# First norm's modulation vectors: full-precision products with the weights stationary, in place of split products with the weights moving

## The chip, the cores and the metric

The kernel runs on one core of one Trainium2 chip. A core has TensorE (PE in the profile, its weight loads PEld), VectorE (DVE), ScalarE (ACT), GpSimd (POOL) and SyncE (SP), which issues most transfers here. The metric is the device time of one execution in microseconds (us); three runs of the kernel before gave 2555.66 to 2558.70 us, median 2557.21 us.

## What is computed

Two transformer blocks over 512 tokens of width 1024. The change lies at the very start of the first block, where two condition vectors (`c` and `c_ctx`, 1024 long each) become the shift and the scale of the first norm:

```python
sh1, sc1, g1, sh2, sc2, g2 = jnp.split(
    (jax.nn.silu(c) @ ada_w[layer] + ada_b[layer])[:, None, :], ADA_CHUNKS, axis=-1)
csh1, csc1, ... = jnp.split(jax.nn.silu(c_ctx) @ ada_w[layer] + ada_b[layer], ADA_CHUNKS, axis=-1)
h = modulate(rmsnorm(x, norm1_g[layer]), sh1, sc1)        # h * (1 + scale) + shift
hc = modulate(rmsnorm(ctx, norm1_g[layer]), csh1, csc1)
q, k, v, gu, gv, ga, gb = jnp.split(h @ w, IN_SPLITS, axis=-1)
```

Of the 6144 columns of `ada_w`, the first 2048 (sh1 and sc1) are used at this place, for both vectors. All later projections need `h`, so nothing of the main work can run before some of it is there. Everything is float32.

## The kernel before

Activations stand transposed: 8 blocks of 128 features, 512 tokens in the free dimension. A large float32 product is made of three products in the reduced type `float32r`: each operand is split into a high and a low part (`split`: ACT rounds, DVE subtracts), and `mm3` (L866 to L869) adds high by high (L867), low by high (L868) and high by low (L869).

The stage in question is the block under `p0` (L972 to L1024). It does three things at once, for feature blocks b = 0 to 7:

- `load(b)` brings 1 MB of ada weights (`ar`: 128 partitions, 8 blocks k of the contraction, 256 columns, which are block b's 128 shift columns and 128 scale columns), and splits it into `ah` and `al`: two instructions of 128x1024 on ACT (L925) and two on DVE (L926).
- `vectors(b, a)` multiplies. The stationary operand is `scp`, 128x4: the high and low parts of silu of the two vectors. The moving operand is 256 columns of `ah` or `al`; 16 products accumulate a 4x256 result (L987, L988). ACT copies it to `asb` (L990), two TensorE transposes turn it (L993), two DVE additions bring the parts and the bias together into `m` (L996, L997), and L998 makes the scale `s`. Then `modulated` makes block b of the activations: `md` on DVE (L947), `hh` on ACT (L948), `hl` on DVE (L949).
- The loop (L1017) multiplies block b of the activations with four weight blocks `wv` (the `gv` columns), 12 products of 512 columns for each b, accumulated over all eight b in four PSUM banks (`ps_mm`, `ps_S`). The four weights are split early by `early` (L1002; two subtractions on POOL, two on DVE).

In program order, vectors(0) and vectors(1) come ahead of the loop, and turn b of the loop holds vectors(b + 2). A scheduler interleaves the instructions of neighbouring turns on each engine, so the order that an engine really follows is shown with the change. Ahead of all stand the sums of squares of x (L913, L918) with two plain float32 products (L920, L922), from which `rfactor` makes the row factor `nR` (L893 to L899). Behind the loop, `gv` is activated from the four banks (L1065), and `proj` (L871) multiplies the next weights (L1071 on).

The buffers of `ar` are three. Further on, at L1045, the kernel makes eight small plain float32 products at a time: stationary a 128x128 block of `modacc`, moving the two columns of `one1`.

Of the kernel before, what the change touches and what calls it, by code (L numbers as in the profile page):

```python
# [8 lines left out]
F32 = mybir.dt.float32  # L9
F32R = mybir.dt.float32r  # L10
# [3 lines left out]
AF = mybir.ActivationFunctionType  # L14
ALU = mybir.AluOpType
# [3 lines left out]
P = 128  # L19
S = 512  # L20
D = 1024
KB = D // P
# [14 lines left out]
V_N1, V_N2, V_FG, V_MIX, V_FFN, V_LN, V_GN, V_AB, V_C, V_SINK = 0, 8, 16, 24, 32, 40, 44, 52, 100, 116  # L37
# [88 lines left out]
def pad(pool, size):  # L126

    pool.tile([P, size // 4], F32, name="pad", bufs=1)
# [695 lines left out]
def body(ctx, tc, I, out):  # L824
    nc = tc.nc
# [16 lines left out]
    vec = cp.tile([P, NVEC], F32, name="vec")  # L842
    nc.sync.dma_start(vec, I["vecs"])
    ident = cp.tile([P, P], F32, name="ident")
# [79 lines left out]
    def split(hi, lo, src):  # L924
        nc.scalar.activation(hi, src, AF.Copy)  # L925
        nc.vector.tensor_sub(lo, src, hi.bitcast(F32))  # L926
# [7 lines left out]
    with ExitStack() as c1:  # L934
        pa = c1.enter_context(tc.tile_pool(name="pa", bufs=1))
        bank = banks(T=(0, 1), mm=(2, 3), S=(4, 5), O=(6, 7))
# [27 lines left out]
        sc = pa.tile([P, KB, 2], F32, name="sc")  # L964
        cv = vec[:, V_C:V_C + 16].rearrange("p (k j) -> p k j", j=2)
        nc.scalar.activation(sc, cv, AF.Silu)
        scp = pa.tile([P, KB, 4], F32R, name="scp")
        split(scp[:, :, 0:2], scp[:, :, 2:4], sc)
        m1 = pa.tile([P, 2, 16], F32, name="m1")
        s1 = pa.tile([P, 2, KB], F32, name="s1")  # L970
        h = (hh, hl)
        with tc.tile_pool(name="p0", bufs=2, side="right") as p0:  # L972

            def load(b):
                ar = p0.tile([P, KB, 2 * P], F32, name="ar", bufs=3)
                nc.sync.dma_start(ar.rearrange("p k c -> p (k c)"), I["adaA"][b])
                ah = p0.tile([P, KB, 2 * P], F32R, name="ah", bufs=2)
                al = p0.tile([P, KB, 2 * P], F32R, name="al", bufs=2)
                for q in range(2):
                    k = slice(q * 4, q * 4 + 4)  # L980
                    split(ah[:, k], al[:, k], ar[:, k])
                return ah, al

            def vectors(b, a):
                acc = bank("O")[:4, :2 * P]
                for k in range(KB):
                    nc.tensor.matmul(acc, scp[:, k, :], a[0][:, k, :], start=k == 0, stop=False)  # L987
                    nc.tensor.matmul(acc[:2], scp[:, k, 0:2], a[1][:, k, :], start=False, stop=k == KB - 1)  # L988
                asb = p0.tile([4, 2, P], F32, name="asb", bufs=2)
                nc.scalar.activation(asb.rearrange("p j c -> p (j c)"), acc, AF.Copy)  # L990
                tp = bank("T")
                for j in range(2):
                    nc.tensor.transpose(tp[:, 4 * j:4 * j + 4], asb[:, j, :], ident[:4, :4])  # L993
                parts = tp[:, 0:8].rearrange("p (j h i) -> p h i j", j=2, h=2)
                m = m1[:, :, b::8]
                nc.vector.tensor_tensor(m, parts[:, 0], vec[:, V_AB + b:V_AB + 16:8].unsqueeze(1).broadcast_to([P, 2, 2]), ALU.add)  # L996
                nc.vector.tensor_tensor(m, m, parts[:, 1], ALU.add)  # L997
                nc.vector.scalar_tensor_tensor(s1[:, :, b], m[:, :, 1], 1.0, gain[:, V_N1 + b:V_N1 + b + 1].broadcast_to([P, 2]),  # L998
                                               op0=ALU.add, op1=ALU.mult)
                modulated(sp, hh, hl, lambda k: xT[:, k, :], S, s1[:, 0, :], R1, m1[:, 0, 0:8], (b,))  # L1000

            def early(b, pool):  # L1002
                raw = wp.tile([P, D], F32, tag="raw", name="raw", bufs=4)
                nc.sync.dma_start(raw, I["win"][b])
                wpool, n = (p0, 2) if b > 17 else (wp, 3)
                hi = wpool.tile([P, D], F32R, tag="hi", name="hi", bufs=n)
                nc.scalar.activation(hi, raw, AF.Copy)
                lo = wpool.tile([P, D], F32R, tag="lo", name="lo", bufs=n)
                (nc.gpsimd if pool else nc.vector).tensor_sub(lo, raw, hi.bitcast(F32))
                return hi, lo  # L1010

            gv_ps = [bank(tag) for tag in ("mm", "mm", "S", "S")]
            vectors(0, load(0))
            wv = [early(16, True), early(17, False)]
            vectors(1, load(1))
            wv += [early(18, True), early(19, False)]
            for b in range(KB):  # L1017
                if b + 2 < KB:
                    a = load(b + 2)
                c = slice(b * P, (b + 1) * P)  # L1020
                for acc, w in zip(gv_ps, wv):
                    mm3(acc, (w[0][:, c], w[1][:, c]), (hh[:, b, :], hl[:, b, :]), b == 0, b == KB - 1)
                if b + 2 < KB:
                    vectors(b + 2, a)  # L1024
# [43 lines left out]
        for b in range(4):  # L1068
            w = weight(I["win"][12 + b])
            acc = bank("mm")  # L1070
# [8 lines left out]
        for n in range(NT):  # L1079
            tp = bank("T")  # L1080
# [182 lines left out]
        x1 = mid.tile([P, KB, S], F32, name="x1")  # L1263
        with tc.tile_pool(name="pm", bufs=1) as pm, tc.tile_pool(name="sr2", bufs=1) as sr:

            pad(pm, 128)
            mh = pm.tile([P, KB, S], F32R, name="mh")
            ml = pm.tile([P, KB, S], F32R, name="ml")
            for b in range(KB):
                if b % 2 == 0:  # L1270
                    wa = weight(I["wpa"][b // 2])
                a_ps = bank("S")
                proj(a_ps, wa, (ya[:, 0], ya[:, 1]), 4, (b % 2) * 4)
                nc.vector.tensor_mul(sga[:, b, :], sga[:, b, :], a_ps)
                nc.vector.tensor_add(sga[:, b, :], sga[:, b, :], gbm[:, b, :])
                split(mh[:, b, :], ml[:, b, :], sga[:, b, :])
            ms, held, R = bank("T"), {}, mid.tile([P, S], F32, name="nR")

            def wout(b, w, c=slice(0, S)):
                acc = bank("mm")[:, :c.stop - c.start]  # L1280
                proj(acc, w, (mh[:, :, c], ml[:, :, c]))
                nc.vector.scalar_tensor_tensor(x1[:, b, c], acc, mod[:, 16 + b:17 + b], x1[:, b, c], op0=ALU.mult, op1=ALU.add)
                squares(sr, ms[:, c], b, x1[:, b, c], held, c)


            late = []
            for b in range(0, KB, 2):
                nc.scalar.dma_start(x1[:, b:b + 2, :], I["xT"][b:b + 2].rearrange("k p t -> p k t"))
            for b in range(KB):
                late.append((b, weight(I["wout"][b])))  # L1290
                if b < KB - 3:
                    wout(*late.pop())
            for half in HALVES:
                for a in late:
                    wout(*a, half)
                rfactor(sr, ms[:, half], S // 2, into=R[:, half], tag="h")
# [16 lines left out]
```

## Time and profile before

| | us |
|---|---|
| Median of three runs (lowest, highest) | 2557.21 (2555.66, 2558.70) |
| The profiled execution | 2557.7 |
| Its span | 2555.9 |
| PE busy | 2476.8 |
| PEld busy | 2135.9 |
| DVE busy | 1787.7 |
| ACT busy | 1065.5 |
| POOL busy | 309.1 |

A busy time is the union of an engine's instructions. Products are pipelined, so one record (0.28 or 0.39 us) is longer than the step from one to the next; what a product costs in a stream is read from the starts. The granted clock of TensorE is given as a share of 2.4 GHz: 1.00 is 2.4 GHz and 0.50 is 1.2 GHz. A view of the waits says what ended an engine's idle time. A plain float32 product leaves two records of a weight load and two of a product.

### The profile page before, as it was taken

How to read it: one execution, taken by the hardware profiler on the slowest of the kernel's cores; microseconds unless marked ns; L12 is line 12 of the kernel's file. 1: busy time of each engine (PE TensorE's matmuls, PEld its weight loads, DVE VectorE, ACT ScalarE, POOL GpSimd, SP SyncE). 2: the span in 40 equal slices, each digit the busy share in tenths (PEclk: the TensorE clock that was granted, in tenths of full speed). 3: DMA queues.
4: the chain of work that ended last, by engine and by line, in shares of the span. 5: the costliest groups of instructions: out<-in, count | busy, mean ns of one | idle time of the engine just before them, and what ended most of it. 6: DMA issues, size and time to landing. Idle time of an engine off the chain costs nothing.

```text
span 2555.9 us, 34576 instructions
## 1 busy us (share of the span) xinstructions
PE 2476.8 (97%) x13153; PEld 2135.9 (84%) x13153; DVE 1787.7 (70%) x2977; ACT 1065.5 (42%) x1846; POOL 309.1 (12%) x200
## 2 busy tenths in 40 slices
PE   7899999999899999999999999999999999999998
PEld 4788888888789999999988888886788888888887
DVE  6656745899989888878888888876854334533345
ACT  6524553433344444444444344344533323422343
POOL 0001100004331111123222222210000000000000
PEclk9999999999899999999999999999999999999999
DMA  6343433224667888799998899972112222222254
GB/s 240 128 173 128 159 106 118 103 83 169 218 245 277 300 294 295 288 347 332 339 344 322 310 358 361 359 292 99 58 50 83 91 101 97 94 96 99 101 182 162
DMA packets 145814, 511.28 MB, mean 200 GB/s; under 512 B 13680, under 2 KB 39408, under 8 KB 125936
## 3 DMA queue, kind: packets, MB, share of 16 engines
q1 hardware_dynamic: 114464, 330.14, 36.9%
q0 software_dynamic: 18432, 134.23, 14.1%
q10 hardware_dynamic: 12752, 44.70, 4.6%
q8 instruction: 103, 1.69, 0.3%
q14 instruction: 63, 0.52, 0.1%
HBM read 465.50 MB, written 43.52 MB: 199 GB/s over the span
## 4 chain that ended last, share of the span: by engine, by line
PE 84%; DVE 11%; issue 2%; ACT 2%; DMA 1%; POOL 0%; DVEq 0%; SPq 0%; ACTq 0%; POOLq 0%
PE ps_mm L867 13%; PE ps_mm L868 12%; PE ps_mm L869 12%; PE ps_o L869 7%; PE ps_o L868 7%; PE ps_o L867 7%; PE ps_S L867 3%; PE ps_S L868 3%; PE ps_S L869 3%; PE ps_S L197 3%; DVE lo L863 2%; PE ps_A L869 1%; PE ps_A L868 1%; PE ps_A L867 1%; PE ps_h L867 1%
## 5 line engine op out<-in xcount | busy, mean ns | idle before, releaser
L863 DVE TENSOR_TENSOR lo<-raw,hi 128x1024 fp32r<-128x1024 f32 x473 | 584.1, 1236 | 372.5 <-ACT hi L861 361.0
L861 ACT ACTIVATE hi<-raw 128x1024 fp32r<-128x1024 f32 x474 | 499.8, 1056 | 755.0 <-PE ps_mm L868 424.6
L869 PE MATMUL ps_mm<-hh,lo 128*128 128x512 f32 (+2 forms) x1784 | 654.5, 367 | 27.2 <-DVE lo L863 27.0
L867 PE MATMUL ps_mm<-hh,hi 128*128 128x512 f32 (+2 forms) x1784 | 661.4, 372 | 7.5 <-ACT gv L1065 2.4
L868 PE MATMUL ps_mm<-hl,hi 128*128 128x512 f32 (+2 forms) x1784 | 655.3, 367 | 2.4 <-DVE hl L926 2.2
L869 PEld LDWEIGHTS ps_mm<-hh,lo 128*128 128x128 f32 x1784 | 339.8, 190 | 65.3 <-DVE lo L863 30.2
L867 PEld LDWEIGHTS ps_mm<-hh,hi 128*128 128x128 f32 x1784 | 339.1, 191 | 45.5 <-ACT gv L1065 2.9
L868 PEld LDWEIGHTS ps_mm<-hl,hi 128*128 128x128 f32 x1784 | 340.1, 191 | 39.1 <-DVE hl L926 3.3
L178 POOL DMA_INDIRECT rows<-in_uv,dix x128 | 217.9, 1702 | 748.2 <-DVE act L427 190.0
L867 PE MATMUL ps_o<-hi,wh 128*128 128x512 f32 x768 | 298.9, 389 | 1.4 <-ACT wh L925 1.4
L869 PE MATMUL ps_o<-hi,wl 128*128 128x512 f32 x768 | 299.7, 390 | 0.6 <-DVE wl L926 0.5
L868 PE MATMUL ps_o<-lo,wh 128*128 128x512 f32 x768 | 299.2, 390 | 0.0
L172 DVE SCALAR_TENSOR_TENSOR rows<-rows,hn 128x1024 f32<-128x1024 f32 x128 | 159.9, 1250 | 18.6 <-ACT act L377 8.3
L869 PEld LDWEIGHTS ps_o<-hi,wl 128*128 128x128 f32 x768 | 144.1, 188 | 31.9 <-DVE wl L926 2.1
L169 DVE SCALAR_TENSOR_TENSOR accn<-rows,wgt,accn 128x1024 f32<-128x1024 f32 x128 | 167.2, 1306 | 4.4 <-ACT wgt L175 2.9
L867 PEld LDWEIGHTS ps_o<-hi,wh 128*128 128x128 f32 x768 | 144.2, 188 | 31.1 <-ACT wh L925 1.7
L868 PEld LDWEIGHTS ps_o<-lo,wh 128*128 128x128 f32 x768 | 144.1, 188 | 29.6
L925 ACT ACTIVATE wh<-act 128x384 fp32r<-128x384 f32 x104 | 54.7, 526 | 240.2 <-PE ps_o L868 219.1
L193 DVE TENSOR_TENSOR gi<-oh,gt 128x1536 bf16<-128x1536 bf16 x96 | 91.3, 954 | 0.9
L191 DVE TENSOR_TENSOR oh<-iob,ji 128x1024 bf16<-128x1024 bf16 x96 | 65.8, 688 | 26.8 <-PE ps_S L197 26.2
L197 PE MATMUL ps_S<-gi,oh 128*128 128x128 bf16 x1152 | 78.1, 219 | 0.0
L868 PE MATMUL ps_S<-hl,hi 128*128 128x512 f32 x200 | 78.0, 390 | 0.0
(398 smaller groups left out, 3589.2 us busy)
## 6 DMA issues: line engine op xcount, KB each, us to landing
raw<-in_uT SPq DMA_DIRECT2D x128, 512.0 KB
raw<-in_uv SPq DMA_DIRECT2D x128, 512.0 KB
raw<-in_win SPq DMA_DIRECT2D x82, 512.0 KB
raw<-in_wd SPq DMA_DIRECT2D x44, 512.0 KB
act<-act ACTq DMA_DIRECT2D x52, 384.0 KB
act<-act SPq DMA_DIRECT2D x52, 384.0 KB
gs<-stage ACTq DMA_DIRECT2D x16, 1152.0 KB
ring<-gs SPq DMA_DIRECT2D x12, 1536.0 KB
```

Source lines behind the costliest of these rows:

```text
L169: nc.vector.scalar_tensor_tensor(accn, rows.pop(k - 3)[:, D:], wgt[:, c], accn, op0=ALU.mult, op1=ALU.add)
L172: paced(nc.vector.scalar_tensor_tensor(r[:, :D], r[:, :D], 1.0, hn, op0=ALU.mult, op1=ALU.mult, accum_out=dot[:, c]))
L178: paced(nc.gpsimd.indirect_dma_start(out=r, out_offset=None, in_=I["uv"], in_offset=bass.IndirectOffsetOnAxis(ap=dix[:, k:k + 1], axis=0)))
L191: nc.vector.tensor_tensor(oh, io, each(ji[:, t0 // 4], 2), ALU.is_equal)
L193: nc.vector.tensor_tensor(gi, oh[:, 1].unsqueeze(1).broadcast_to([P, 3, 2, P, 2]), each(gt[:, t0 // 4], 3), ALU.mult)
L197: nc.tensor.matmul(g_ps[:, t, :], oh[:, 0, t // 2, :, t % 2], gi[:, j, t // 2, :, t % 2], start=j == 0, stop=j == 2)
L861: nc.scalar.activation(hi, raw, AF.Copy)
L863: (nc.gpsimd if pool else nc.vector).tensor_sub(lo, raw, hi.bitcast(F32))
L867: nc.tensor.matmul(ps, w[0], x[0], start=first, stop=False)
L868: nc.tensor.matmul(ps, w[0], x[1], start=False, stop=False)
L869: nc.tensor.matmul(ps, w[1], x[0], start=False, stop=last)
L925: nc.scalar.activation(hi, src, AF.Copy)
```

## The change

The ada weights of this stage are no longer split. They stay float32 and become the stationary operand, a 128x128 block at a time; the moving operand is the two columns of `sc` (silu of `c` and `c_ctx`), also float32. The result comes out with features on the partitions, two columns for the shift and two for the scale, so the copy to `asb` and the transposes are gone, and one addition is left. For each b there are again 16 products (8 contraction blocks, 2 halves). `scp` is gone with its split; a filler tile of 128 bytes further on (`pad(pm, 128)`) is taken out, which offsets the space that `scp` took.

```diff
-        scp = pa.tile([P, KB, 4], F32R, name="scp")
-        split(scp[:, :, 0:2], scp[:, :, 2:4], sc)
 ...
             def load(b):
                 ar = p0.tile([P, KB, 2 * P], F32, name="ar", bufs=3)
                 nc.sync.dma_start(ar.rearrange("p k c -> p (k c)"), I["adaA"][b])
-                ah = p0.tile([P, KB, 2 * P], F32R, name="ah", bufs=2)
-                al = p0.tile([P, KB, 2 * P], F32R, name="al", bufs=2)
-                for q in range(2):
-                    k = slice(q * 4, q * 4 + 4)
-                    split(ah[:, k], al[:, k], ar[:, k])
-                return ah, al
+                return ar
 
             def vectors(b, a):
-                acc = bank("O")[:4, :2 * P]
-                for k in range(KB):
-                    nc.tensor.matmul(acc, scp[:, k, :], a[0][:, k, :], start=k == 0, stop=False)
-                    nc.tensor.matmul(acc[:2], scp[:, k, 0:2], a[1][:, k, :], start=False, stop=k == KB - 1)
-                asb = p0.tile([4, 2, P], F32, name="asb", bufs=2)
-                nc.scalar.activation(asb.rearrange("p j c -> p (j c)"), acc, AF.Copy)
-                tp = bank("T")
+                acc = bank("O")
                 for j in range(2):
-                    nc.tensor.transpose(tp[:, 4 * j:4 * j + 4], asb[:, j, :], ident[:4, :4])
-                parts = tp[:, 0:8].rearrange("p (j h i) -> p h i j", j=2, h=2)
+                    for k in range(KB):
+                        nc.tensor.matmul(acc[:, 2 * j:2 * j + 2], a[:, k, j * P:(j + 1) * P], sc[:, k, :],
+                                         start=k == 0, stop=k == KB - 1)
                 m = m1[:, :, b::8]
-                nc.vector.tensor_tensor(m, parts[:, 0], vec[:, V_AB + b:V_AB + 16:8].unsqueeze(1).broadcast_to([P, 2, 2]), ALU.add)
-                nc.vector.tensor_tensor(m, m, parts[:, 1], ALU.add)
+                nc.vector.tensor_tensor(m, acc[:, 0:4].rearrange("p (j i) -> p i j", j=2),
+                                        vec[:, V_AB + b:V_AB + 16:8].unsqueeze(1).broadcast_to([P, 2, 2]), ALU.add)
 ...
-            pad(pm, 128)
```

The scheduler orders the stage anew. On TensorE at the start of the program (`sqs` and `sq` belong to the sums of squares), the kernel before has

```order
L920 MATMUL ps_T<-sqs,ones 128x512
L922 MATMUL ps_T<-sq,ones 128x512
L987 MATMUL ps_O<-ah,scp 4x256
L988 MATMUL ps_O<-al,scp 2x256
```

and the changed one has

```order
L920 MATMUL ps_T<-sqs,ones 128x512
L922 MATMUL ps_T<-sq,ones 128x512
L981 MATMUL ps_O<-sc,ar 128x2 x32
L867 MATMUL ps_mm<-hh,hi 128x512 x2
L867 MATMUL ps_S<-hh,hi 128x512
```

The 32 small products of vectors(0) and vectors(1) now stand in one row ahead of the first main product; before, 32 split products stood there, with two transposes between.

In the middle of the loop, still on TensorE, the turn b = 4 of the changed kernel reads

```order
L867 MATMUL ps_mm<-hh,hi 128x512 x2
L867 MATMUL ps_S<-hh,hi 128x512 x2
L981 MATMUL ps_O<-sc,ar 128x2 x16
L868 MATMUL ps_mm<-hl,hi 128x512
L869 MATMUL ps_mm<-hh,lo 128x512
L868 MATMUL ps_mm<-hl,hi 128x512
L869 MATMUL ps_mm<-hh,lo 128x512
L868 MATMUL ps_S<-hl,hi 128x512
```

where three more of the main products follow and then the next turn begins. The block of 16 small products for turn b + 1 stands inside turn b; behind it stand 10 main products in turn 1, 9 in turns 2 and 3, 8 in turn 4, 7 in turn 5 and 8 in turn 6. Turns 0 and 7 have no such block. Before, the split products of one vector were spread over two turns, and the transposes came after them in the next.

On VectorE at the start, the kernel before has the left-over splits of the ada weights (`al`) between the steps of the row factor (`nt`, `nR`):

```order
L897 SCALAR_TENSOR_TENSOR nt<-ps_T,nt 128x512
L926 TENSOR_TENSOR al<-ar,ah 128x1024
L899 SCALAR_TENSOR_TENSOR nR<-nt,nr 128x512
L926 TENSOR_TENSOR al<-ar,ah 128x1024
L947 SCALAR_TENSOR_TENSOR md<-xT,s_143,nR 128x512
```

and the changed one has

```order
L897 SCALAR_TENSOR_TENSOR nt<-ps_T,nt 128x512
L984 TENSOR_TENSOR m_139<-ps_O,vec 128x4
L899 SCALAR_TENSOR_TENSOR nR<-nt,nr 128x512
L986 SCALAR_TENSOR_TENSOR s_140<-m_139,gain 128x2
L947 SCALAR_TENSOR_TENSOR md<-xT,s_140,nR 128x512 x2
```

The second `m`, which reads the result of vectors(1), now stands ahead of `nR`. Two more places move: the first later weight split on VectorE (`lo`) stands between `md` and `hl` of the last block, and on SyncE the loads of `ar` now wait for TensorE to have read the buffer, where they waited for VectorE's split before.

## Rows read from the trace of the kernel before

**Rows 1.** By stretch: its us, then busy us (x instructions) of PE, PEld, DVE, ACT, POOL; clock, DMA.

```profile
16.00:28.70 12.70, 4.86 (x27) 2.33 (x26) 8.84 (x10) 9.28 (x12) 3.78 (x2) 0.74 0.67 253
28.70:65.40 36.70, 36.69 (x203) 26.25 (x202) 28.11 (x50) 19.92 (x28) 0.00 (x0) 0.95 0.48 183
```

**Rows 2.** Timeline of the start: start us, us, engine line op tiles [idle before, releaser].

```profile
13.06 1.92 PE L922 MATMUL ps_T<-sq,ones 128*128 128x512 f32 x2
...
21.49 0.68 DVE L897 SCALAR_TENSOR_TENSOR nt<-ps_T,nt 128x512 f32<-128x512 f32 x1
...
23.23 0.68 DVE L899 SCALAR_TENSOR_TENSOR nR<-nt,nr 128x512 f32<-128x512 f32 x1
...
27.27 0.37 PE L988 MATMUL ps_O<-al,scp 128*2 128x256 f32 x1 [2.04 <-DVE al L926]
...
28.69 0.50 PEld L867 LDWEIGHTS ps_mm<-hh,hi 128*128 128x128 f32 x2 [0.27 <-ACT hh L948]
```

**Rows 3.** The chain that ended last, behind the loop: start us, us, what.

```profile
65.43 0.92 issue
...
69.36 0.50 PE ps_mm L867
```

**Rows 4.** Timeline of PE around eight plain products with two moving columns.

```profile
142.58 0.40 PE L868 MATMUL ps_mm<-hl,hi 128*128 128x512 f32 x1
142.81 1.85 PE L1045 MATMUL ps_O<-one,modacc 128*128 128x2 f32 x16
144.52 0.48 PE L869 MATMUL ps_mm<-hh,lo 128*128 128x512 f32 x1
...
145.07 0.39 PE L868 MATMUL ps_mm<-hl,hi 128*128 128x512 f32 x1
...
147.79 0.39 PE L868 MATMUL ps_S<-yb,hi 128*128 128x512 f32 x1
```

**Rows 5.** Timeline of PE: two split products that stand sixteen steps apart.

```profile
33.55 0.28 PE L987 MATMUL ps_O<-ah,scp 128*4 128x256 f32 x1
...
35.40 0.28 PE L987 MATMUL ps_O<-ah,scp 128*4 128x256 f32 x1
```

**Rows 6.** Timeline around the last vectors, as in Rows 2.

```profile
61.38 0.28 PE L993 MATMUL ps_T<-ident,asb 4*128 4x4 f32 x2
61.70 0.17 DVE L996 TENSOR_TENSOR m<-ps_T,vec 128x4 f32<-128x4 f32 x1 [2.16 <-PE ps_T L993]
61.90 0.16 DVE L997 TENSOR_TENSOR m<-m,ps_T 128x4 f32<-128x4 f32 x1
62.10 0.16 DVE L998 SCALAR_TENSOR_TENSOR s<-m,gain 128x2 f32<-128x2 f32 x1
62.29 0.75 DVE L947 SCALAR_TENSOR_TENSOR md<-xT,s,nR 128x512 f32<-128x512 f32 x1
63.08 0.72 ACT L948 ACTIVATE hh<-md,m 128x512 fp32r<-128x512 f32 x1 [1.87 <-DVE md L947]
```

**Rows 7.** Groups: line engine op tiles xcount | busy us, mean ns | idle before, releasers.

```profile
L925 ACT ACTIVATE ah<-ar 128x1024 fp32r<-128x1024 f32 x16 | 16.1, 1045 | 4.6 <-PE ps_O L987 2.6 <-DMA ar<-in_adaA 1.3 <-ACT ah L925 0.7
...
L863 DVE TENSOR_TENSOR lo<-raw,hi 128x1024 fp32r<-128x1024 f32 x10 | 12.1, 1219 | 13.1 <-ACT hi L861 13.1
```

**Rows 8.** By stretch, as in Rows 1, and a timeline row of the last L1045 block.

```profile
70.00:72.00 2.00, 2.00 (x6) 1.63 (x5) 0.38 (x2) 1.76 (x6) 0.00 (x0) 0.50 1.13 390
72.00:74.00 2.00, 2.00 (x7) 1.58 (x7) 1.62 (x4) 1.64 (x6) 0.00 (x0) 0.68 1.02 410
319.00:321.00 2.00, 2.00 (x16) 1.51 (x14) 1.37 (x2) 0.98 (x3) 1.52 (x1) 1.00 1.08 268
321.00:323.00 2.00, 2.00 (x17) 1.91 (x18) 1.08 (x3) 0.69 (x3) 0.00 (x0) 1.00 0.68 207
...
319.83 1.95 PE L1045 MATMUL ps_O<-one,modacc 128*128 128x2 f32 x16
```

**Rows 9.** Timeline of ACT and DVE where PE next runs dry.

```profile
109.03 1.06 ACT L861 ACTIVATE hi<-raw 128x1024 fp32r<-128x1024 f32 x1 [1.28 <-PE ps_mm L868]
```

## The prediction

> **What bounds the kernel now.** I read first the busy times by stretch, because the change touches one stage, and a share over the whole program says nothing about it. From 28.7 to 65.4 us TensorE is busy for 36.69 of 36.70 us, VectorE for 28.11 and ScalarE for 19.92 [rows 1]. So the loop is bound by TensorE alone: the splits that the change removes there lie beside work that is longer. It is different ahead of the loop. From 16.0 to 28.7 us TensorE is busy for 4.86 of 12.70 us [rows 1], and the timeline says what it waits for: a split product begins at 27.27 after 2.04 us of waiting for a split on VectorE, and the first weight load of the main products comes at 28.69 [rows 2]. Here the splits are on the path. Behind the loop the chain of waits goes from the end of the last products at 65.43 over ScalarE to the next product at 69.36 [rows 3]; the changed order leaves that piece as it is, so what counts is when the loop ends.
>
> The change thus trades in two places: it shortens the path to the first main product, and it puts other small products into a loop that has no room on TensorE.
>
> **The change part by part.**
>
> *What a new product costs.* The same form stands in the trace already: L1045 multiplies a plain float32 128x128 block with two moving columns. One 512-column product starts at 142.58, the eight small ones follow at 142.81, and the next large one starts at 144.52 [rows 4]. Large products stand 12 steps apart between 145.07 and 147.79 [rows 4], so a step is 0.227 us. The eight cost 144.52 - 142.58 - 0.23 = 1.71 us, or 0.107 us for each of 16 records. `vectors` has 16 such products: 3.42 us. Before, sixteen steps of split products took 35.40 - 33.55 = 1.85 us [rows 5], and the two transposes 0.28 us as a record [rows 6], some 0.25 in the stream: 2.10 us. So a vector gets dearer on TensorE by 1.32 us, though it no longer needs two passes of splitting.
>
> *The start.* The float32 products of the sum of squares end at 13.06 + 1.92 = 14.98 [rows 2]. Behind them stand 32 small products in a row: 2 x 3.42, to 21.8. Their weights need no split any more, only the transfer, for which ScalarE's first split waited 1.3 us in all [rows 7]; I take it as landed. Then, in VectorE's new order, `m` 0.17, `nR` 0.68, `s` 0.16, `md` 0.75, then `hh` 0.72 on ScalarE [rows 2, 6], and six handovers of some 0.04 us (0.03 from `m` to the next, 0.04 from `md` to `hh` [rows 6]): 24.5 us. The other input of this chain is the row factor: `nt` ended at 22.17 before [rows 2] behind splits that are now gone, so it ends at 22.2 at the latest, about when `m` is there, and cannot delay the chain by more than 0.2 us. First main product at 24.5 where it was 28.7: **-4.2 us**.
>
> *The loop.* Six vectors stand in it: 6 x 1.32 = **+7.9 us**. Nothing hides this, since TensorE was full.
>
> *The handover from vector to activations.* From the end of the small products, the path to the next `hh` was 61.66 to 63.80 [rows 6], 2.14 us; one addition (0.20 with its gap) falls away, and releasing TensorE adds some 0.05: 2.0 us. What covers it is the main products that stand behind the block in the same turn: 10, 9, 9, 8, 7 and 8 of them at 0.227 us, which is 2.27, 2.04, 2.04, 1.82, 1.59 and 1.82 us. Three turns fall short, by 0.2, 0.4 and 0.2. In the last turn `hl` stands behind `md` and a weight split of 1.22 us [rows 7] on VectorE, so it is ready 2.0 us after `md`; TensorE begins the turn 0.8 us after `md` and has four products (0.9) without it: 0.3 us. Together **+1.1 us**, between 0 and 2.
>
> *The clock.* In the loop before, the granted clock averaged 0.95 [rows 1]; 0.05 of 36.7 us is 1.8 us lost, at its start, after idle. In the changed kernel TensorE sits idle from 21.8 to 24.5. After the idle stretch of 4 us that ends at 69.36 the clock was 0.50 for 2 us and averaged 0.68 over the next 2 [rows 3, 8]: 1.0 + 0.6 = 1.6 us lost. For 2.7 us of idle I take 1.0, between 0 and 1.6: **-0.8 us** against before.
>
> *SyncE.* The loads of `ar` now wait for TensorE's reading in place of VectorE's split. With three buffers, the sixth load goes out when vectors(2) is done, and its data is wanted three turns of some 6 us later; what queues behind it on SyncE is the next weights, wanted after the loop. Nothing, as long as turns are not shorter than a transfer.
>
> *The sum*: -4.2 + 7.9 + 1.1 - 0.8 = +4.0 us. The loop ends at 69.4 and everything behind it moves along. The profiled execution took 2557.7 us, so 2561.7; it lay 0.5 us above the median of the three runs, so I expect **2561.2 us** beside 2557.2. The parts alone allow +1.9 (no handover stall, no half clock) to +6. A measurement of this kernel can tell about 0.2% (5.1 us) from no change, so the likeliest result is no change that can be told, on the slow side of it.
>
> **The rivals.**
>
> *The clock falls in the small blocks (slower).* A record of 0.107 us here is nearly all weight load, with two columns streaming. If that does not keep the clock up, TensorE goes to 1.2 GHz during the two vectors at the start and again in the loop. The price: vectors(1) at half clock takes 3.4 us more; six falls in the loop, each as dear as the one behind the loop (1.6 us [rows 8]), are 9.6; the 1.0 already counted goes off: 4.0 + 3.4 + 9.6 - 1.0 = +16, or 2573.2 us, and more if it stays low (half the loop's 42 us at half clock would be +21). It decides as soon as one block of 3.42 us brings the clock down. Against it: an L1045 block begins at 319.83, its records last 1.95 us, and the clock is 1.00 from 319 to 323 [rows 8]. For it: that block is half as long, the 32 in a row at the start are four times as long, and no row shows such a stretch. The Trainium skill's page "TensorE: Matmul & The Clock Gate", section "Part 4: PE-mode transpose", says of transposes that they do not count as a busy TensorE for the clock as products do; whether a product of two columns counts, it does not say, and no row here isolates it. Chance 0.20.
>
> *The weight loads hide (faster).* In the loop before, the weight port was busy for 26.25 of 36.70 us [rows 1]. If the new loads slipped into its 10.4 free us, beneath the 512-column products, the sum would be 4.0 - 10.4 = -6.4, or 2550.8 us. Rows 4 speak against it: there, too, large products stood on both sides, and every record cost its 0.107 us. The same page, section "Back-to-back issue gap", gives a floor of about 25 ns from start to start for up to 64 moving columns, and says that weight loads are left out of it; 32 records at 25 ns would be an estimated 0.8 us a vector and a kernel some 12 us faster, but the trace's 0.107 us decides. Chance 0.05.
>
> *The delay is swallowed later.* TensorE next runs dry behind a weight split on ScalarE at 109.03. If that split, and the work queued behind it, did not depend on when the loop ended, 4 us would vanish there: 2557.2 us. But it comes after 1.28 us of idle time that a main product ended [rows 9]. So it moves along. Chance 0.07.
>
> **How the numbers follow.** My forecast has 0.68: 0.47 of it within 0.2% and 0.21 above, when stalls, clock and start all come out at their dear ends. The clock rival is nearly all slower (0.19 of 0.20, the rest no change), the hidden loads are faster (0.05), the swallowed delay is no change (0.07). That makes faster 0.05, same 0.55, slower 0.40. The range leaves out the hidden loads below and the worse half of the clock rival above: 2556.5 to 2574 us.
>
> **What would show it.** In the changed kernel's profile: the first main product near 24.5 us; 32 records of L981 in a block of 3.4 us in six turns; the last main product of the loop near 69; granted clock 1.00 through the blocks; idle time of TensorE ended by `hh` in turns 4 to 6, some tenths each. Records of L981 at 0.21 us steps would prove the clock rival, blocks well under 3.4 us the hidden loads, and a first main product later than 26 us would break the start.

## The result: slower, and the profile after

The changed kernel takes 2580.10 us in the median of six runs (2577.55 to 2585.21) where the kernel before took 2558.14 beside it (six runs, 2555.66 to 2561.08): a ratio of 1.0088, with a 95% interval from 1.0075 to 1.0101. That is 22 us slower, outside my range and far from the 2561.2 us that I forecast. What came true is the rival that I gave 0.20: the clock falls in the small blocks.

| us | before | after |
|---|---|---|
| Profiled execution | 2557.7 | 2585.2 |
| Its span | 2555.9 | 2583.3 |
| PE busy | 2476.8 | 2506.9 |
| DVE busy | 1787.7 | 1767.9 |
| ACT busy | 1065.5 | 1047.8 |

The profiled execution of after is the longest of its six, so its 27.4 us of added span are some 5 us more than the median shows. VectorE and ScalarE lost the work that the change takes away, 20 and 18 us. TensorE, the engine that bounds this stage, gained 30 us of busy time.

The stretches answer to [rows 1] and have the same columns; the one before the last is the clock:

```profile
14.00:19.00 5.00, 5.00 (x37) 4.48 (x36) 0.15 (x1) 3.99 (x5) 2.34 (x1) 1.00 1.01 413
19.00:27.70 8.70, 6.32 (x31) 6.24 (x30) 4.22 (x10) 3.24 (x6) 2.35 (x1) 0.50 0.65 245
27.70:91.70 64.00, 63.98 (x284) 56.22 (x285) 14.66 (x28) 7.10 (x10) 0.00 (x0) 0.64 0.27 99
...
34.00:36.00 2.00, 2.00 (x20) 2.00 (x19) 0.00 (x0) 0.00 (x0) 0.00 (x0) 1.00 0.00 0
36.00:38.00 2.00, 2.00 (x10) 1.98 (x10) 0.29 (x2) 0.00 (x0) 0.00 (x0) 0.53 0.00 0
38.00:40.00 2.00, 2.00 (x6) 1.54 (x5) 1.18 (x3) 0.72 (x1) 0.00 (x0) 0.50 0.67 168
...
95.70:102.00 6.30, 6.30 (x29) 5.20 (x28) 2.85 (x7) 5.01 (x13) 0.00 (x0) 1.00 0.89 311
```

The loop now runs from 27.7 to 92.9 us (the third row has all of it but the last 1.2 us), and TensorE is busy in all of it. What has changed is the clock: a mean of 0.64, where it was 0.95. The rows from 34 to 40 show one fall close up; the last row lies behind the loop and is used further below. Inside a block of small products 20 records pass in 2 us at clock 1.00; in the next 2 us the block ends at about half that rate, and the main products behind it still run at 0.50, though TensorE has not been idle for a moment.

The timeline answers to [rows 2, 3] (start us, us, instruction, idle time and its releaser):

```profile
14.77 10.55 PE L981 MATMUL ps_O<-sc,ar 128*128 128x2 f32 x64
...
25.36 0.17 DVE L984 TENSOR_TENSOR m<-ps_O,vec 128x4 f32<-128x4 f32 x1 [4.06 <-PE ps_O L981]
25.44 0.68 DVE L899 SCALAR_TENSOR_TENSOR nR<-nt,nr 128x512 f32<-128x512 f32 x1
...
27.71 1.22 PE L867 MATMUL ps_mm<-hh,hi 128*128 128x512 f32 x2 [2.39 <-ACT hh L948]
...
33.33 4.30 PE L981 MATMUL ps_O<-sc,ar 128*128 128x2 f32 x32
...
79.12 6.82 PE L981 MATMUL ps_O<-sc,ar 128*128 128x2 f32 x32
...
92.54 0.40 PE L869 MATMUL ps_S<-hh,lo 128*128 128x512 f32 x1
...
95.37 0.49 PE L867 MATMUL ps_mm<-hh,hi 128*128 128x512 f32 x1 [2.43 <-ACT gv L1053]
```

In the timeline of before, the first and the last main product of the loop are:

```profile
28.72 1.19 PE L867 MATMUL ps_mm<-hh,hi 128*128 128x512 f32 x2
...
66.53 0.39 PE L869 MATMUL ps_S<-hh,lo 128*128 128x512 f32 x1
```

Six blocks of 32 records stand in the loop, as forecast, but they last from 3.84 to 6.82 us in place of 3.4: the last runs wholly at half clock. From the first main product to the next product behind the loop it is 95.37 - 27.71 = 67.66 us, where before it was 69.36 - 28.72 = 40.64 (69.36 from [rows 3]): **+27.0 us**. The clock takes 64.0 x 0.36 = 23.0 us of that stretch against 36.7 x 0.05 = 1.8 before: 21.2. This counts everything at 0.50 as twice as slow, which takes a little too much: the step of the main products there is 0.43 us, against 0.23. The other 5.8 are the small products themselves, since the gap behind the last main product is 2.43 us in both. The start gives back 1.0 us only (27.7 against 28.7). So the stage accounts for 26.0 of the 27.4 us.

### The profile page after: what moved, and what is told of

Same layout as the page of the kernel before. It is cut to its first block, busy times and chain, and to the rows that moved or that the text cites. A ratio compares the mean times of both kernels' runs of the same rounds, so it can differ in the third digit from the quotient of the medians.

```text
span 2583.3 us, 34738 instructions
## 1 busy us (share of the span) xinstructions
PE 2506.9 (97%) x13265; PEld 2172.3 (84%) x13265; DVE 1767.9 (68%) x2952; ACT 1047.8 (41%) x1821; POOL 307.2 (12%) x200
## 4 chain that ended last, share of the span: by engine, by line
PE 85%; DVE 10%; ACT 2%; DMA 1%; issue 1%; POOL 0%; DVEq 0%; SPq 0%; ACTq 0%; POOLq 0%
PE ps_mm L867 12%; PE ps_mm L869 12%; PE ps_mm L868 12%; PE ps_o L869 7%; PE ps_o L868 7%; PE ps_o L867 7%; PE ps_S L868 3%; PE ps_S L869 3%; PE ps_S L867 3%; PE ps_S L197 3%; DVE lo L863 2%; PE ps_A L868 2%; PE ps_A L869 2%; PE ps_A L867 2%; PE ps_O L981 1%
## 5 line engine op out<-in xcount | busy, mean ns | idle before, releaser
L869 PE MATMUL ps_mm<-hh,lo 128*128 128x512 f32 (+2 forms) x1784 | 656.9, 369 | 28.7 <-DVE lo L863 28.6
L867 PEld LDWEIGHTS ps_mm<-hh,hi 128*128 128x128 f32 x1784 | 340.2, 191 | 47.6 <-ACT gv L1053 2.9
L868 PEld LDWEIGHTS ps_o<-lo,wh 128*128 128x128 f32 x768 | 144.5, 188 | 29.6
L869 PE MATMUL ps_S<-hh,lo 128*128 128x512 f32 x200 | 80.8, 404 | 0.0
```

What stands on the lines that cost most here:

```text
L867: nc.tensor.matmul(ps, w[0], x[0], start=first, stop=False)
L868: nc.tensor.matmul(ps, w[0], x[1], start=False, stop=False)
L869: nc.tensor.matmul(ps, w[1], x[0], start=False, stop=last)
```

## The experiments

In each, "the next product" is the first one behind the loop: 69.36 us in before, 95.37 in after.

### Is it the clock, and what lets it fall?

**Wide columns (e1_wide).** The same products with the same weights, but the two columns are repeated to 128; all else is the changed kernel, except that the scheduler now puts each block at the head of its turn.

```diff
-nc.tensor.matmul(acc[:, 2 * j:2 * j + 2], a[:, k, j * P:(j + 1) * P], sc[:, k, :],
+nc.tensor.matmul(acc[:, 128 * j:128 * j + 128], a[:, k, j * P:(j + 1) * P],
+                 sc[:, k, :].unsqueeze(1).broadcast_to([P, 64, 2]),
```

> Edit: the changed kernel, but each small product streams 128 columns (the two columns of silu repeated 64 times) in place of 2; the same weight loads, more columns, the same result. Theory (the clock falls because two columns beneath a weight load do not keep it up): the step stays near 0.107 us a record since the weight load still sets it, the granted clock stays at 1.00 in the loop, the loop ends near 69 us in place of 92.8, and the time is 2558 to 2564 us, some 18 us under the changed kernel. Rival (the small products cost what they cost, whatever the clock does to them): more columns can only add, the clock still falls, 2580 us or more.

It took 2565.34 us (before beside it 2557.75), ratio 1.0032 (1.0021 to 1.0043), a little above the 2558 to 2564 of the theory. Its stretches, with the columns of [rows 1]:

```profile
26.00:30.00 4.00, 3.88 (x10) 3.06 (x11) 3.07 (x6) 1.74 (x3) 0.00 (x0) 0.57 0.27 109
30.00:71.00 41.00, 41.00 (x279) 37.21 (x278) 13.07 (x27) 7.03 (x9) 0.00 (x0) 1.00 0.40 144
```

And two of its blocks in the timeline:

```profile
30.57 3.73 PE L981 MATMUL ps_O<-sc,ar 128*128 128x128 f32 x32
...
36.91 3.73 PE L981 MATMUL ps_O<-sc,ar 128*128 128x128 f32 x32
```

After one low stretch at its start the loop runs at 1.00 to its end, with 64 times the columns and the same number of weight loads. A turn is 36.91 - 30.57 = 6.34 us; twelve main products at 0.227 are 2.72, so a vector costs 3.62, near the 3.42 that I had taken from [rows 4]. The next product starts at 73.69: 4.3 us later than before, where my sum said 4.0. That these two are so close is in part luck: the first main product came at 26.12, 1.6 later than forecast, and the stall of 1.1 did not come. But the price of the products was right, and the clock was the error: of the changed kernel's 22 us, 14 to 15 go when the columns become more.

**Half the products (e2_half).** Two columns again, but only the shift's eight products for each vector; the scale's are left out and the shift stands in for it.

```diff
-for j in range(2):
+for j in range(1):
```

> Edit: the changed kernel with half of the small products: the scale's 8 products of each vector are left out (the shift is used for both, so the computation is not the reference's). Blocks of 8 in the loop, as L1045 has them. Theory (clock): blocks of 1.7 us between twelve large products leave the clock at 1.00 in most of the loop, as around L1045, so the loop shrinks by far more than half of the added products: it ends near 58 us, time near 2548. Rival (a fixed price for each product, about 0.26 us as measured in the changed kernel): half the products save half of the blocks' time, some 18 us, time near 2562, with the clock still falling in most turns.

One run of 2560.75 us, near the time of the rival and 12 us above that of the theory, though the clock did what the theory says. In its timeline, a block and a wait of a main product:

```profile
31.05 1.84 PE L981 MATMUL ps_O<-sc,ar 128*128 128x2 f32 x16
...
49.90 0.73 PE L867 MATMUL ps_mm<-hh,hi 128*128 128x512 f32 x2 [0.27 <-ACT hh L948]
```

And the loop's stretch:

```profile
31.00:61.00 30.00, 29.12 (x172) 24.34 (x172) 11.00 (x24) 5.29 (x7) 0.00 (x0) 1.00 0.47 176
```

Blocks of this size, in turns of 5.1 us, leave the clock at 1.00. This is what [rows 4, 8] had shown me around L1045; it does not carry over to the changed kernel's blocks. The run halves the blocks and their part of a turn together, and so does not say which of the two counts. The last main product ends at 63.1 us, where I had expected 58, and the next product comes at 65.58, 3.8 us earlier than in before. Yet the one execution took 3.0 us more than the median of before beside it; this I can't explain. The wait of 0.27 us for `hh` comes three times: the handover stall of my sum, which the changed kernel's slow TensorE hides.

**Longer blocks elsewhere (e7_later_blocks).** The kernel before, with L1045's eight products made twice in its first two blocks and four times in its last two, some 75 to 270 us behind the loop.

```diff
-for b in range(KB):
+for b in list(range(KB)) * (2 if j < 2 else 4):
     nc.tensor.matmul(am[:, 2 * b:2 * b + 2], acc[:, b * P:(b + 1) * P], one1, start=True, stop=True)
```

> The kernel before with the four later blocks of L1045 made longer, outside the stage of the change: the eight products are made twice in the first two blocks and four times in the last two (the extra results are overwritten). A row of before shows clock 1.00 around eight (1.71 us). Theory (a block of 16, 3.4 us, is long enough to bring the clock down, in any surroundings): the clock is at 0.50 for some microseconds in or behind each of the four blocks, weight loads of the second half of the blocks of 32 take 0.34 us in place of 0.19, and the blocks of 32 take well over their 6.85 us. Rival (the fall belongs to the first stage, with its start from an idle TensorE): clock 1.00 throughout, blocks of 3.4 and 6.85 us.

The first and the third block in the timeline:

```profile
143.90 4.75 PE L1045 MATMUL ps_O<-one,modacc 128*128 128x2 f32 x32
...
281.69 9.81 PE L1045 MATMUL ps_O<-one,modacc 128*128 128x2 f32 x64
```

The clock in and behind the four blocks, by stretch:

```profile
144.00:146.00 2.00, 2.00 (x21) 2.00 (x19) 0.56 (x1) 0.00 (x0) 0.00 (x0) 1.00 0.85 313
...
146.00:154.00 8.00, 8.00 (x29) 6.87 (x29) 1.31 (x2) 1.21 (x2) 0.00 (x0) 0.57 0.53 168
234.00:240.00 6.00, 6.00 (x35) 5.37 (x35) 1.99 (x3) 0.79 (x3) 0.00 (x0) 0.72 0.33 128
...
286.00:296.00 10.00, 10.00 (x46) 9.51 (x46) 1.99 (x3) 0.60 (x1) 0.00 (x0) 0.51 0.11 30
344.00:354.00 10.00, 10.00 (x48) 9.81 (x47) 0.86 (x2) 1.20 (x2) 0.00 (x0) 0.51 0.05 21
```

All four blocks bring the clock down, in a part of the program where it stands at 1.00 in before. The one run took 2587.45 us, 29.6 more than before beside it. The added products are 2 x 1.71 + 2 x 5.13 = 13.7 us at full clock; the two stretches of 10 us at 0.51 lose 9.8, and those of 8 and 6 us around the ends of the shorter blocks 3.4 and 1.7: the sum is 28.6. So the fall belongs to these products, not to the first stage or to its idle start.

**Only the loop (e5_loop_narrow).** Vectors 0 and 1 are split as before; vectors 2 to 7 are made by two-column products.

```diff
 def vectors(b, a):
+    if b in (2, 3, 4, 5, 6, 7):
+        acc = bank("O")
+        for j in range(2):
+            for k in range(KB):
+                nc.tensor.matmul(acc[:, 2 * j:2 * j + 2], a[:, k, j * P:(j + 1) * P], sc[:, k, :],
+                                 start=k == 0, stop=k == KB - 1)
...
+    else:
         acc = bank("O")[:4, :2 * P]
```

> The kernel before with vectors(2) to vectors(7) by the two-column products; vectors(0) and vectors(1) are split as before, so the start is that of before (first main product near 28.7 us). Theory (each unbroken block of two-column products in the loop brings the granted clock down by itself): falls of the clock in or behind the blocks of the loop, as in the changed kernel, whose loop took 27 us more than before from its first main product to the next product behind it; that product near 96 us, a time of 2578 to 2585 us. Rival (the 64 records at the start bring the clock down, and the loop only inherits that): clock 1.00 through the loop's blocks once it has risen, the next product near 78 us (69.4 + 7.9 + 1.1), a time near 2567 us.

2581.41 us, ratio 1.0098 (1.0082 to 1.0113): as slow as the whole change. Its profiled execution is the quickest of four (2578.4 us). By stretch:

```profile
22.00:49.00 27.00, 23.78 (x88) 19.41 (x88) 11.02 (x16) 5.03 (x7) 2.38 (x1) 0.50 0.27 100
49.00:63.00 14.00, 14.00 (x100) 12.94 (x99) 3.67 (x8) 1.45 (x2) 0.00 (x0) 0.99 0.51 185
63.00:70.00 7.00, 7.00 (x24) 5.89 (x24) 1.83 (x4) 0.72 (x1) 0.00 (x0) 0.53 0.58 232
...
77.00:87.00 10.00, 10.00 (x61) 8.47 (x59) 3.71 (x6) 2.66 (x3) 0.00 (x0) 1.00 0.16 52
```

Two of its blocks in the timeline:

```profile
53.99 3.63 PE L992 MATMUL ps_O<-sc,ar 128*128 128x2 f32 x32
...
77.78 3.63 PE L992 MATMUL ps_O<-sc,ar 128*128 128x2 f32 x32
```

The next product came at 89.12, between the theory's 96 and the rival's 78. The start was not quite that of before: some products of vectors(2) stood ahead of the first main product, which came at 31.48. The clock fell after 14 us at 0.99, so the loop's blocks do it by themselves, and the 64 records at the start are not needed for the loss. But two things are not as the theory has them. Not each block brings the clock down: the two shown above run at full rate, and the clock is still 1.00 in the main products behind them. And in the first row the clock also fails to *rise*, for 17.5 us from the first main product on, while small products and main products alternate.

**The same products, spread (e6_spread, e11_spread_wide).** To see whether long unbroken blocks are the cause, I cut each vector's 16 products into four groups of four and pinned two or three main products (`main`) behind each group (`products`); the second of these runs has 128 columns in place of two.

```diff
+for q in range(4):
+    if b + 2 < KB:
+        products(o, a, q, pin)
+    for n in range(q < 3, 3):
+        main(q, n)
```

> The changed kernel with the 16 two-column products of a vector cut into four groups of four, and two or three 512-column products pinned between the groups; work and share of the small products in a turn stay as they are (3.4 of some 6.1 us). Theory (an unbroken run of 3.4 us of two-column products is what brings the clock down): clock 1.00 through the loop once it has risen, the next product behind the loop at 75 to 78 us where the changed kernel had 95.4, a time of 2563 to 2567 us. Rival (their share in a turn is what counts, wherever they stand): the clock falls as in the changed kernel, next product near 95 us, a time near 2580 us.

> The run with the small products in four groups of four between pinned main products, now with 128 moving columns in place of two. Theory (two columns to a weight load are what leaves the clock at 0.50 there, not the cutting or the pinned order): clock 1.00 through the loop once it has risen, 45 to 48 us from the first main product to the next one behind the loop, a time of 2562 to 2567 us. Rival (frequent change between small and large products, or the pinned order, is the cause): the clock stays at 0.50 as with two columns, some 78 us, a time near 2600 us.

Two columns: 2599.13 us, ratio 1.0162 (1.0148 to 1.0176), the slowest of all; the next product came at 108.83, later than theory and rival had it. 128 columns: 2569.33 us, ratio 1.0031 (1.0018 to 1.0043), the median 2 us above the theory's range. The loop with two columns, by stretch:

```profile
44.00:48.00 4.00, 4.00 (x31) 3.71 (x29) 0.43 (x1) 0.00 (x0) 0.00 (x0) 0.97 0.46 193
48.00:102.00 54.00, 54.00 (x196) 48.41 (x196) 10.20 (x21) 4.56 (x6) 0.00 (x0) 0.50 0.22 80
```

And with 128:

```profile
29.00:70.80 41.80, 41.77 (x277) 37.55 (x275) 13.63 (x27) 7.25 (x10) 0.00 (x0) 1.00 0.38 139
```

My theory fell here. With the small products in groups of 0.9 us the clock does not stay up: it is 0.97 for 4 us and then 0.50 for 54, without a break. So no unbroken block is needed. Cut up, the products even cost more: from the first main product to the next one behind the loop it is 108.83 - 30.88 = 77.95 us, against 67.66 in the changed kernel. In that kernel the clock rose again in the stretches of main products alone, which are missing here; that this is the reason is likely, but not shown. The same order with 128 columns runs at 1.00 and takes 73.01 - 25.63 = 47.4 us to the next product, as in e1_wide (47.6): neither the cutting nor the pinned order costs anything there. What the pair e6 and e11 changes is only the number of moving columns for each weight load; after and e1_wide differ in that and in the place of the blocks. So the number of columns decides here; why it does, no run shows.

### Where did the gain at the start go?

**The start alone (e3_start_wide, e4_start_narrow).** Vectors 0 and 1 by the new products, with 128 columns and with two; the rest split as before. The edit of the first (the second has two columns there):

```diff
+    if b in (0, 1):
+        acc = bank("O")
+        for j in range(2):
+            for k in range(KB):
+                nc.tensor.matmul(acc[:, 128 * j:128 * j + 128], a[:, k, j * P:(j + 1) * P],
+                                 sc[:, k, :].unsqueeze(1).broadcast_to([P, 64, 2]), start=k == 0, stop=k == KB - 1)
...
+    else:
         acc = bank("O")[:4, :2 * P]
```

> Edit: the kernel before, with vectors 0 and 1 alone by plain products, 128 columns streamed; vectors 2 to 7 split as before. Theory (the path to the first main product ran over the splits, and the loop had no room): the first main product comes near 24.5 us in place of 28.7 and the loop is as long as before, so 3 to 5 us faster than the kernel before, near 2554. Rival (the splits for vectors 2 and 3 now arrive later and the loop waits for them): no gain, 2557 to 2560.

> Edit: as e3, but vectors 0 and 1 with two columns, as in the changed kernel. Theory (clock): the clock falls in the row of 32, vectors(1) takes some 6 us, the first main product comes near 27.5 us at 1.2 GHz, so at best 1 us faster than the kernel before, 2556 to 2559. Rival (the block at the start has no effect on the clock): as e3, near 2554.

With 128 columns 2556.76 us, ratio 0.9995 (0.9986 to 1.0004): no difference. With two 2561.00, ratio 1.0013 (1.0003 to 1.0022), 2 us above the theory's range; the first main product came at 30.92, not 27.5, because all 64 records ran at half clock (see the last section). With 128 columns the first main product came at 25.41 us, 0.9 later than my 24.5. Its timeline says why:

```profile
21.43 2.62 POOL L1021 TENSOR_TENSOR lo<-raw,hi 128x1024 fp32r<-128x1024 f32 x1 [4.69 <-ACT hi L1019]
21.89 2.71 DVE L947 SCALAR_TENSOR_TENSOR md<-xT,s,nR 128x512 f32<-128x512 f32 x1
```

`md` takes 2.71 us there, and 0.75 elsewhere [rows 6]. It began while GpSimd subtracted the low part of a weight, and ended 0.55 us after that did. The same stands in the trace of before: `al` takes 3.38 us beside GpSimd's `lo`, and 1.2 elsewhere:

```profile
23.76 2.37 POOL L1009 TENSOR_TENSOR lo<-raw,hi 128x1024 fp32r<-128x1024 f32 x1 [6.35 <-ACT hi L1007]
...
23.83 3.38 DVE L926 TENSOR_TENSOR al<-ar,ah 128x1024 fp32r<-128x1024 f32 x1
```

The Trainium skill's page "SBUF — State Buffer", section "SBUF: two separate sides", says that a VectorE instruction with two inputs from SBUF and a GpSimd instruction that reads SBUF share a pair of ports as an exclusive lock, so that the later of the two waits to the end of the earlier. The rows agree: 23.76 + 2.37 is 26.13, and 1.2 us of work behind it end at 27.3, where `al` ended at 27.21. In e3_start_wide 21.43 + 2.62 is 24.05, and 0.75 behind it 24.80, where `md` ended at 24.60.

That is one part. The first main product is 3.3 us earlier than in before, but the next product, at 67.25, only 2.1. Most of the rest goes to the clock: behind the long wait for `md` it is low at the start of the loop.

```profile
24.00:31.00 7.00, 5.59 (x13) 4.44 (x14) 5.19 (x8) 4.41 (x6) 0.05 (x1) 0.54 0.31 126
```

**Without GpSimd beside it (e8_start_no_pool, e9_before_no_pool).** One word moves that split to VectorE, in e3_start_wide and in the kernel before:

```diff
-wv += [early(18, True), early(19, False)]
+wv += [early(18, False), early(19, False)]
```

> The earlier run with vectors(0) and vectors(1) by 128-column products and the others split, in which the first md took 2.71 us on VectorE while GpSimd subtracted a weight's low part (alone it takes 0.75); here that third early weight split goes to VectorE behind md. Theory (GpSimd's subtraction beside it is what stretches md, and that is why the first main product came 1.6 us later than I forecast): md 0.75 us, first main product near 23.5 us where it was 25.4, next product behind the loop near 65.3 us, a time 2 us below that run's 2556.8. Rival (the row factor or the products set this time, or the split now standing ahead of hl gives the gain back): first main product at 25 us or later, or the loop ending where it did, a time near 2556.8 us.

> The kernel before with the third early weight split on VectorE in place of GpSimd, and nothing else. Theory (the gain of the run with this edit was that of taking GpSimd's subtraction away from beside VectorE's work, whoever makes the vectors): the split al that took 3.38 us at 23.83 us in before takes 1.2, the first main product comes near 26.6 us where it was 28.7, the next product behind the loop near 67.2 us, a time near 2555.7 us. Rival (it pays only where the vectors come early; here VectorE's own splits bound the start, and 1.2 us more of them stands in the same row): first main product at 28 us or later, a time of 2557 to 2559 us.

Both are faster than before: 2553.35 us, ratio 0.9981 (0.9971 to 0.9990), and 2553.90 us, ratio 0.9981 (0.9972 to 0.9989). The timeline of e8_start_no_pool:

```profile
21.97 0.75 DVE L947 SCALAR_TENSOR_TENSOR md<-xT,s,nR 128x512 f32<-128x512 f32 x1
...
23.53 0.74 PE L867 MATMUL ps_mm<-hh,hi 128*128 128x512 f32 x2 [0.97 <-ACT hh L948]
```

And of e9_before_no_pool:

```profile
24.85 1.22 DVE L926 TENSOR_TENSOR al<-ar,ah 128x1024 fp32r<-128x1024 f32 x1
...
27.54 0.74 PE L867 MATMUL ps_mm<-hh,hi 128*128 128x512 f32 x2
```

Their loops, by stretch, e8_start_no_pool first:

```profile
23.00:61.00 38.00, 36.74 (x204) 25.70 (x204) 30.31 (x51) 22.74 (x30) 0.00 (x0) 1.00 0.50 185
...
28.00:66.00 38.00, 36.32 (x206) 25.58 (x204) 29.91 (x52) 22.14 (x30) 0.00 (x0) 1.00 0.46 177
```

The stretch is gone in both, and the theory holds for `md` and `al`. In e8 the next product comes at 63.19 us, 2.1 earlier than I expected. In e9 it comes at 67.22 as expected, but by another way: the first main product moved only to 27.54 (not 26.6), and the rest came in the loop. In both loops the clock is 1.00, where before had a mean of 0.95: with the shorter wait ahead of it, TensorE loses less to the clock too. Yet both kernels take the same time in the end, so the 4 us by which e8 is ahead do not show there. The end of e9's loop moved 2.1 us, and its median 4.4. Such differences of some microseconds between the end of the loop and the whole I have not settled; the executions of the kernel before alone range from 2554.57 to 2562.26 us. For the same reason the median of e11_spread_wide, 4 us above that of e1_wide, shows no difference: the ratios to before are 1.0031 and 1.0032.

### The change with both corrections

**128 columns, and no GpSimd beside md (e10_wide_no_pool).** The two edits above on the changed kernel.

> All eight vectors by 128-column products, as in the earlier run, and the third early weight split on VectorE. Theory (with the clock up and md not stretched, the two terms of my sum stand: the start some 4 to 5 us earlier, the loop 7 us dearer): no fall of the clock before the loop, first main product at 23.5 to 24.5 us, next product behind the loop at 69 to 70.5 us where before had 69.35, a time of 2560 to 2562 us, about what I forecast for the changed kernel. Rival (the start is bound by the products of vectors(0) and vectors(1) and cannot come earlier than 26 us): next product near 73 us, a time near 2565 us as in that run.

Its loop, by stretch:

```profile
23.50:67.50 44.00, 43.94 (x288) 39.23 (x288) 16.80 (x33) 9.10 (x12) 0.00 (x0) 1.00 0.46 165
```

2561.52 us, ratio 1.0017 (1.0008 to 1.0026). The first main product comes at 23.57, the next one at 69.73, and the clock is 1.00 through the loop. My sum of +4.0 at this point, less the stall of 1.1, the 1.0 of half clock and the 0.9 by which the start is earlier, would be +1.0; it is +0.4. So with the clock held up the terms add up in the stage to within 0.6 us, though I chose which terms to take off after I had seen the runs. That the time is also about the 2561.2 that I forecast for the change is luck: the stage ends 0.4 us later than in before, not 4.0, and some 3 us come behind it, for which I have no cause. Against e9_before_no_pool the new products start the loop 4.0 us earlier and take 6.5 more in it, and the kernel takes 7.6 us more. In no run is a kernel with them measurably faster than the same kernel with split ones.

## Why the prediction was wrong, step by step

- **What bounds the kernel** was right: TensorE is busy without a gap in the loop, before and after, so VectorE's and ScalarE's 38 us of saved work bought nothing there.
- **What a new product costs** was right at clock 1.00: 3.62 us a vector in e1_wide against 3.42. The rival by which the weight loads hide fell with it.
- **The clock** is the step that failed. It said -0.8 us against before, with 1.0 lost after an idle gap, and counted a clock loss for idle time alone. In the changed kernel 23.0 us go in the loop at a TensorE that is never idle, because two-column products stand in it. For the rival I had the price near (half the loop at half clock, +21; the traces say 21.2 more than before), but I put it behind a smaller price of six short falls, which gave 2573.2, and gave the case 0.20.
- The price of an idle gap rested on a wrong reading. 65.43 in [rows 3] is not the end of the last products, and TensorE was not idle for 4 us ahead of 69.36: the last product ended at 66.53 + 0.39 = 66.92, so it was 2.44. A gap of 2.4 us cost 1.6 there; a gap of 2.43 at the same place of the changed kernel cost nothing (clock 1.00 from 95.70 on). The length of the gap alone does not set this price.
- Why the chance was too low: the only row for it was L1045's block, with clock 1.00 around 1.71 us of such products between main ones [rows 4, 8]. I read it as speaking against the rival. It spoke of a block half as long, standing alone; e7 doubled that very block, and the clock fell. In the loop of the changed kernel a block of twice that length stands in six turns. The prediction itself says that no row of before shows such a stretch, and should have given the rival more for it. The Trainium skill's page "TensorE: Matmul & The Clock Gate", section "Part 4: PE-mode transpose", says of transposes alone that they do not count for the clock as products do. These runs show that two-column products, each with its own weight load, do not hold it either in this loop: 0.64 with two columns, 1.00 with 128 in e1_wide.
- **The start**: 27.7 us in place of 24.5. The block of 64 records took 10.55 us, as the clock was 0.50 in part of it, and the second `m` stands ahead of `nR` on VectorE, so the row factor waited for it until 25.44. With the clock up (e1_wide, e3_start_wide) the first main product was held by GpSimd instead; with both gone it came at 23.5. The 3.38 us of `al` stood in the trace of before, and I did not ask why one split took so long.
- **The loop**, +7.9: right in size, somewhat too dear. In the changed kernel 5.8 are left when the clock's part is taken off. With 128 columns, from the first main product to the next one it is 46.16 us in e10 against 40.64 before, +5.5; before lost another 1.8 to its clock there, so the products' own share is 7.3.
- **The handover**, +1.1: not seen in the changed kernel, where the main products at half clock give it more cover. It shows in e2_half as three waits of 0.27 us.
- **SyncE** was right: no wait of TensorE for a transfer in the loop. **The delay swallowed later** did not come: 26.0 us at the next product, 27.4 at the end.

## What to carry over

Before products of a few columns with fresh weights each take the place of wide ones in a stretch that TensorE bounds, price the stretch at both levels of the clock, and don't take a short block of the kind that stands alone as evidence for a stream of them. Repeating the moving operand to more columns is a cheap test of it, since the weight loads stay the same. Here it also took the clock's loss away, though the kernel stayed slower than before. Where one instruction of a kind takes three times its usual time, look at what the other engines do in that moment before you use its duration in a sum.

## What the runs showed of the hardware that I had not expected

**A clock of 1.00 ahead of its first change need not be one.** In e4_start_narrow the stretch from 14 to 28 us is listed with clock 1.00, and yet each weight load of its 64 records takes 333 ns, as at 0.50 in after, and not 190 (the line's loads: least, median and most ns; then the stretch):

```profile
L992 PEld LDWEIGHTS ps_O<-sc,ar x64: 333/333/337, 14.0 to 28.1; 128*128 128x128 f32 x64
...
14.00:28.00 14.00, 14.00 (x65) 13.47 (x63) 4.03 (x4) 6.56 (x8) 4.69 (x2) 1.00 0.70 280
```

So TensorE ran these products at half clock, and they did not raise it for 14 us. The durations tell it; the listed clock does not. e6_spread starts in the same way (333 ns, and a listed clock of 1.00 up to 44 us). In the changed kernel the same block rose to full rate for some 3 us and fell again (the listed clock falls at 19), so executions differ in this.

**The clock can stay down with a busy TensorE for 54 us** (e6_spread): no idle time is needed for it.

**A VectorE instruction can wait inside its own duration**: `md` 2.71 us for 0.75, `al` 3.38 for 1.2, both beside a GpSimd subtraction.
